# State space operators built in the first mixer's stage instead of the first, with norm sums and modulation steps in turn

## Chip, core and metric

The program runs on one NeuronCore of a Trainium2 chip. The time is the device time of one execution in microseconds (us), median over several. A profiled execution gives the trace; its engines are PE (TensorE matmul) and PEld (its weight loads), DVE (VectorE), ACT (ScalarE), POOL (GpSimd) and SP (SyncE, which here only issues DMAs; ACT and POOL issue some too).

## What is computed

Two networks run one after the other on 256 tokens of width 1024, all in float32. The first has two transformer blocks with adaptive modulation, the second an S5 state space block and an attention block. The parts that matter here are these:

```python
# first network, block i: modulation from the condition, for latent and context tokens
mod = silu(c) @ ada_w[i] + ada_b[i]            # 1024 x 6144; six vectors sh1 sc1 ga1 sh2 sc2 ga2
u   = rms_norm(h, g_mix[i]) * (1 + sc1) + sh1  # input of the mixer (block 0: neighborhood attention)
h   = h + ga1 * (mixer(u) @ wo)
h   = h + ga2 * squared_relu_mlp(rms_norm(h, g_mlp[i]) * (1 + sc2) + sh2)

# second network, S5 mixer: 64 groups of 16 channels, 64 complex states
a_bar = exp(lam * dt)                          # per group and state
b_bar = ((a_bar - 1) / lam)[..., None] * b_mat
s_t   = a_bar * s_{t-1} + b_bar u_t            # scan over the tokens
y_t   = real(c_mat s_t) + d_skip * u_t
```

The S5 scan is computed over chunks of eight tokens. For that the kernel builds operators from `lam`, `dt`, `b`, `c` and `d` alone, independent of the tokens: powers of `a_bar` times `b_bar` (`e`), their transposes (`et`), the short convolution kernel `c a^k b` with `d` on its diagonal (`k1`, `k2`), and some more.

## The kernel before, in words

Every product of the two networks is a float32 product split in two: a weight part of 128 x 1024 is loaded into `raw` (L266, L268), ACT rounds it to `whi` (L109), DVE subtracts to get `wlo` (L112), and PE runs three matmuls per pair of tiles (L294 to L296, or L302 to L304). `whi` and `wlo` have four buffers each, `raw` two.

Stages follow each other as blocks of `_build`, each with its own pools in SBUF and PSUM:
- The first stage (L936 to L1020) loads inputs and constants, sets up S5 (`S5.__init__` L599, `tables` L689, `c` L704), transposes x and ctx into `h` and `hc` (L983), runs 16 modulation steps (`ada`, `ada_steps` L345: load 128 x 1024 of `ada_w`, four matmuls L360 into one PSUM tile; at the eighth step of each vector a copy to `adacc`, two transposes and the bias), computes the norm's sums (`rstd` L442: eight squares, each summed by matmuls L428), and normalises (`normed` L466: per tile `t` on DVE, `xh` on ACT, `xl` on DVE). It also builds the operators for r = 0 to 3: `e(r)` is twelve DVE instructions, `operators(r)` is `k1`, `et` and `k2` on PE and ACT; `et` writes to DRAM (`edr`). At its end `zero` and `k_out` (16 DMAs of SP) write the convolution kernel to DRAM (`kdr`), and `save` some setup (`cdr`).
- From L975 to L1010 stands `tc.manual_schedule`: inside, every engine's instructions keep the order of the program. Outside, the framework orders them with its own planner, which may move an instruction of an engine past others; the eight `spread` DMAs (L794), written in the MLP's stage at L1259, are issued from 169.5 us on, in the attention's stage.
- The first mixer (L1028 to L1197) interleaves chains of scores and softmax with the products of the next head pair and with modulation steps; the bias tiles `bt` are loaded by SP from `rpad` (L1125).
- The next stage (L1240 to L1269) has the rest of the mixer's output product, the second norm of the block, the MLP on 512 tokens (32 weight tiles, after each of which two modulation steps run), and the S5 work that needs no tokens: `reload` of the setup from `cdr` on SP behind a small POOL instruction that waits for the last `h`, `phases` and sixteen `f` on POOL, and `spread`.
- The S5 layer itself (L1494 on) loads `edr`, `fdr`, `tdr` and `vdr`.

Of the kernel before, what the change touches and what calls it, by code (L numbers as in the profile page):

```python
# [17 lines left out]
KT = 8  # L18
# [64 lines left out]
def _build(ctx, tc, I, out, dbg):  # L83
# [337 lines left out]
    def rstd_rows(n, pooled=6, late=KT - 2):  # L421
# [20 lines left out]
    def rstd(n, pooled=6, late=KT - 2, tag="x"):  # L442

        return spread_cols(rstd_rows(n, pooled, late), n, tag)
# [123 lines left out]
    cdr = dram.tile([128, 1632], F32, name="cdr")  # L568
# [6 lines left out]
    def s5_load(pp):  # L575
        lt = spare(4, "lt")[0:32].rearrange("p (i n) -> p i n", i=4)
        ld = pp.tile([32, 2], F32, name="ld")
        dr = pp.tile([32, 32], F32, name="dr")
        bt = [[pp.tile([128, 1024], F32, tag=f"e{1 + r}{j}", name=f"bt{r}{j}")[0:32] for j in range(2)]
              for r in range(2)]  # L580
        ci = [pp.tile([128, 1024], F32, tag=f"e3{i}", name=f"ci{i}").rearrange("p (b d n) -> p b d n", b=8, d=2)
              for i in range(2)]
# [3 lines left out]
        for r, nm in ((0, "a_b_re_2"), (1, "a_b_im_2")):  # L586
            for j in range(2):
                todo.append((bt[r][j], I[nm][0].rearrange("(g j) p h -> g j (p h)", j=2)[:, j]))
# [3 lines left out]
        todo.append((dr, I["a_d_2"][0].rearrange("(a b) -> a b", b=32)))  # L592
        return (lt, ld, dr, bt, ci), [
            lambda o=o, i=i, n=n: (G.dma_start if 7 <= n < 11 else dma_a)(out=o, in_=i) for n, (o, i) in enumerate(todo)]

    class S5:


        def __init__(self, pp, loads):  # L599
            self.pp = pp  # L600
            lt, ld, dr, bt, ci = loads
# [11 lines left out]
            for r in range(2):  # L613
                for j in range(2):
# [15 lines left out]
            def sin_arg(t1, x, t0):  # L630
# [17 lines left out]
            cbs = spare(5, "cbk")  # L648
            G.memset(cbs, 0.0)
            self.cbk = [cbs[:, 256 * i:256 * i + 256].rearrange("p (q a b h) -> p q a b h", q=4, a=2, b=2)  # L650
                        for i in range(2)]
# [34 lines left out]
            self.ci, self.dr = ci, dr  # L686
            self.u, self.t_ = [(cs, sn), (s_[7], s_[8])], (t0, t1)

        def tables(self):  # L689
# [9 lines left out]
            self.em = [[pp.tile([128, 1024], F32, tag=f"e{r}{i}", name=f"e{r}{i}").rearrange(  # L699
                "p (q j t h) -> p q j t h", q=4, j=2, t=8) for i in range(2)] for r in range(3)]  # L700
            self.tm = [spare(2 + i, f"tm{i}").rearrange("p (n t h) -> p n t h", n=4, t=8) for i in range(2)]
            self.kt = [None] * 4

        def c(self):  # L704
            pp, ct, ci, dr = self.pp, self.ct, self.ci, self.dr
# [10 lines left out]
            for r in range(2):  # L716
                act(self.pf_[:, r], self.pw[r][:, 1:9, :], AF.Copy)
            self.dd = dd = pp.tile([32, 32, 32], F32, name="dd")
            pdk = bank("s")
            T.transpose(pdk[0:32, 0:32], dr, ident[0:32, 0:32])  # L720
            act(dr, pdk[0:32, 0:32], AF.Copy)
            tt(dd, dr.unsqueeze(2).to_broadcast([32, 32, 32]), ident[0:32, 0:32].unsqueeze(1).to_broadcast([32, 32, 32]),
               MUL)
            self.kst = [spare(10 + i, f"kst{i}").rearrange("p (r q j x) -> p r q j x", r=4, q=2, j=2) for i in range(2)]
            self.em.append([pp.tile([128, 1024], F32, tag=f"e3{i}", name=f"e3{i}").rearrange(
                "p (q j t h) -> p q j t h", q=4, j=2, t=8) for i in range(2)])

        def save(self):
# [12 lines left out]
        def k1(self, r):  # L741
# [6 lines left out]
            kp = bank("s")  # L748
# [9 lines left out]
            self.kt[r] = kt_ = self.pp.tile([128, 256], F32, tag="kt", name="kt", bufs=2)  # L758
# [13 lines left out]
        def k2(self, r):  # L772
            pk = bank("s")
# [24 lines left out]
        def reload(self, fp):  # L798
            c = fp.tile([128, 1632], F32, name="c")
            tt(c[:, 0:1], h[KT - 1][:, 0:1], hc[KT - 1][:, 0:1], ADD, G)  # L800
# [3 lines left out]
            self.ph = c[:, 1536:1632].rearrange("p (i g) -> p i g", i=3)  # L804

# [118 lines left out]
    with ExitStack() as sa:  # L924
# [11 lines left out]
        with ExitStack() as s0:  # L936
# [32 lines left out]
            def operators(r):  # L969
                s5.k1(r)  # L970
                s5.et(r)
                s5.k2(r)

# [928 lines left out]
```

## Time and profile before

| | us |
|---|---|
| median of three runs (1772.63 to 1781.13) | 1774.6 |
| the profiled execution | 1774.26 |
| its span, first to last instruction | 1772.5 |
| PE busy in the span | 1684.8 (95%) |
| DVE, ACT, POOL busy | 1177.6, 797.4, 445.7 |

A row of the timeline tells when an instruction (or a run of equal ones) started, how long it took, engine, source line, operation, output tile <- input tiles and shape; in brackets the idle time of the engine before it and what ended that. A row of the stretches tells the busy time of each engine in a window, the number of instructions, the granted clock of PE as a share of full, and the share of the 16 DMA engines. Matmuls are pipelined: their lengths overlap, so the distance of two starts tells what one of them costs.

### The profile page before, as it was taken

To read this page: it belongs to the slowest core of one execution; us is meant where nothing else is said; L and a number is where in the kernel's file an instruction comes from. 1 tells how busy PE (TensorE), PEld (TensorE's weight loads), DVE (VectorE), ACT (ScalarE), POOL (GpSimd) and SP (SyncE) were. 2 spreads that over 40 slices of the span, in tenths; PEclk is the share of its full clock that TensorE was granted. 3 is DMA by queue.
4 is the path that set the end of the run, shared out by engine and by line. 5 is a ranking of instruction groups with operands and counts; after the bars stand their busy time and mean duration, and the time that the engine had idled before them with its cause. 6 is when DMAs were issued, how large, how long until landed. Compare 5 with 4: busy or idle time off the path is not lost. (4 is left out here: it accounts for less than half of the span.)

```text
span 1772.5 us, 33896 instructions
## 1 busy us (share of the span) xinstructions
PE 1684.8 (95%) x13257; PEld 1485.2 (84%) x13257; DVE 1177.6 (66%) x2412; ACT 797.4 (45%) x1463; POOL 445.7 (25%) x619
## 2 busy tenths in 40 slices
PE   6899999999999999998998999989899999999999
PEld 5687888876677777888878999979899999789998
DVE  6877777855545333447985756768577788957674
ACT  5544444434323131324674635536444465544453
POOL 4022112146897000040002000221431322424130
PEclk9899999999999999999999999999999999999999
DMA  9566455333766555332206666698459574335952
GB/s 283 180 161 193 123 153 169 91 112 130 238 197 214 160 173 151 87 95 72 84 25 167 189 187 186 209 310 228 129 149 247 146 224 143 108 103 166 233 160 90
DMA packets 428288, 286.57 MB, mean 162 GB/s; under 512 B 37513, under 2 KB 405336, under 8 KB 428128
## 3 DMA queue, kind: packets, MB, share of 16 engines
q1 hardware_dynamic: 422064, 271.53, 52.8%
q0 software_dynamic: 2800, 7.29, 1.3%
q10 hardware_dynamic: 3264, 5.59, 0.9%
q8 instruction: 104, 1.70, 0.4%
q14 instruction: 56, 0.46, 0.1%
HBM read 271.41 MB, written 17.15 MB: 163 GB/s over the span
## 5 line engine op out<-in xcount | busy, mean ns | idle before, releaser
L109 ACT ACTIVATE whi<-raw 128x1024 fp32r<-128x1024 f32 (+2 forms) x388 | 390.1, 1013 | 470.4 <-PE g L295 361.5
L112 DVE TENSOR_TENSOR wlo<-raw,whi 128x1024 fp32r<-128x1024 f32 (+2 forms) x388 | 466.1, 1207 | 186.3 <-ACT whi L109 182.7
L296 PE MATMUL g<-xh,wlo 128*128 128x256 f32 (+1 forms) x1216 | 372.8, 307 | 8.0 <-DVE wlo L112 8.0
L294 PE MATMUL g<-xh,whi 128*128 128x256 f32 (+1 forms) x1216 | 371.9, 307 | 1.6 <-ACT xh L109 1.2
L295 PE MATMUL g<-xl,whi 128*128 128x256 f32 (+1 forms) x1216 | 371.5, 305 | 0.0
L294 PE MATMUL g<-oh,whi 128*128 128x256 f32 (+1 forms) x1056 | 333.2, 316 | 3.5 <-ACT oh L109 1.4
L296 PE MATMUL g<-oh,wlo 128*128 128x256 f32 (+1 forms) x1056 | 333.0, 315 | 0.0
L295 PE MATMUL g<-ol,whi 128*128 128x256 f32 (+1 forms) x1056 | 332.6, 315 | 0.4 <-DVE ol L112 0.4
L296 PEld LDWEIGHTS g<-xh,wlo 128*128 128x128 f32 x1216 | 232.2, 191 | 21.5 <-DVE wlo L112 10.2
L294 PEld LDWEIGHTS g<-xh,whi 128*128 128x128 f32 x1216 | 231.6, 191 | 17.6 <-ACT whi L109 3.9
L295 PEld LDWEIGHTS g<-xl,whi 128*128 128x128 f32 x1216 | 231.8, 191 | 10.9
L294 PEld LDWEIGHTS g<-oh,whi 128*128 128x128 f32 x1056 | 198.2, 188 | 24.2 <-issue 3.7
L295 PEld LDWEIGHTS g<-ol,whi 128*128 128x128 f32 x1056 | 198.3, 188 | 15.8 <-DVE ol L112 1.2
L296 PEld LDWEIGHTS g<-oh,wlo 128*128 128x128 f32 x1056 | 199.4, 189 | 14.3 <-issue 0.2
L302 PE MATMUL g<-whi,xh 128*128 128x256 f32 x560 | 163.1, 292 | 3.9 <-ACT whi L109 1.6
L303 PE MATMUL g<-wlo,xh 128*128 128x256 f32 x560 | 157.9, 282 | 0.1
L304 PE MATMUL g<-whi,xl 128*128 128x256 f32 x560 | 156.9, 283 | 0.2 <-DVE xl L115 0.2
L115 DVE SCALAR_TENSOR_TENSOR h<-g,mods,h 128x256 f32<-128x256 f32 x64 | 30.9, 483 | 142.2 <-PE g L296 142.2
L302 PEld LDWEIGHTS g<-whi,xh 128*128 128x128 f32 x560 | 105.9, 189 | 12.8 <-issue 8.7
L109 ACT ACTIVATE oh<-t 128x256 fp32r<-128x256 f32 (+1 forms) x108 | 51.3, 482 | 124.4 <-DVE t L112 124.4
L303 PEld LDWEIGHTS g<-wlo,xh 128*128 128x128 f32 x560 | 105.9, 189 | 0.8 <-issue 0.3
L304 PEld LDWEIGHTS g<-whi,xl 128*128 128x128 f32 x560 | 105.4, 189 | 1.3 <-issue 0.8
(329 smaller groups left out, 2823.4 us busy)
## 6 DMA issues: line engine op xcount, KB each, us to landing
raw<-mlp_w SPq DMA_DIRECT2D x128, 512.0 KB, 4.3
ada<-ada_w SPq DMA_DIRECT2D x88, 512.0 KB, 5.0
raw<-ffn_w_up SPq DMA_DIRECT2D x88, 512.0 KB, 5.2
raw<-ffn_w_down SPq DMA_DIRECT2D x32, 384.0 KB, 3.8
raw<-ffn_w_down SPq DMA_DIRECT2D x32, 320.0 KB, 3.4
raw<-na_wqkv SPq DMA_DIRECT2D x32, 256.0 KB, 5.0
raw<-a_w_glu SPq DMA_DIRECT2D x16, 512.0 KB, 7.2
raw<-w_kv SPq DMA_DIRECT2D x16, 512.0 KB, 3.7
```

What stands on the lines that cost most here:

```text
L109: last[0] = A.activation(out=o, in_=i, func=f, **kw)
L112: (e or V).tensor_tensor(out=o, in0=a, in1=b, op=op)
L115: V.scalar_tensor_tensor(out=o, in0=a, scalar=s, in1=b, op0=op0, op1=op1)
L294: T.matmul(ps, lhsT=a, rhs=xh[k][:, s0:s1], start=first, stop=False)
L295: T.matmul(ps, lhsT=a, rhs=xl[k][:, s0:s1], start=False, stop=False)
L296: T.matmul(ps, lhsT=b, rhs=xh[k][:, s0:s1], start=False, stop=last_)
L302: T.matmul(ps, lhsT=xh[k][:, t0:t0 + 128], rhs=a, start=first, stop=False)
L303: T.matmul(ps, lhsT=xh[k][:, t0:t0 + 128], rhs=b, start=False, stop=False)
L304: T.matmul(ps, lhsT=xl[k][:, t0:t0 + 128], rhs=a, start=False, stop=last_)
```

## The change

- In the first stage the operators are gone. It keeps the setup (`S5.__init__`, `tables`, `c`), and `save` now also writes `bb` and `pw2` to `cdr`, which grows from 1632 to 3168 columns. `b` is loaded with one DMA for each of its two parts (two before) and turned with 16 transposes each (16 transposes and 16 matmuls before). The loads of `c` and the small loads stand ahead of `tables`.
- `rstd` takes a function `between`, called after each of the eight sums: here it runs one modulation step each time, with `prep_vectors` at the fifth. Then `c`, four steps, the first weights, four steps. The second weights are loaded behind.
- `normed` of the first mixer now stands inside the hand-ordered section.
- `reload` stands at the head of the stage that holds the output product and the MLP. It loads the larger `cdr` without the POOL instruction that waited for `h`, loads `d` and builds `dd`, and allocates the operators' tiles: one `em` for all r, two `et` in turn (four before).
- `e(0)` follows `reload`; `k1`, `et` and `k2` of r = 0 stand behind the output product, ahead of the norm. Those of r = 1 to 3 hang on modulation steps of the MLP: `e` at steps 24, 32 and 40, the others four to six steps later, `k_out` at step 47; the eight `spread` follow behind all modulation steps.

```diff
@@ rstd_rows
+            if between:
+                between()
@@ S5.__init__
-                for j in range(2):
-                    b_ = bt[r][j].rearrange("g (p h) -> g h p", h=16)
-                    for h_ in range(16):
-                        o_ = pb[r][64 * j:64 * j + 64, 32 * h_:32 * h_ + 32]
-                        if j:
-                            T.matmul(o_, lhsT=b_[:, h_, :], rhs=ident[0:32, 0:32])
-                        else:
-                            T.transpose(o_, b_[:, h_, :], ident[0:32, 0:32])
+                b_ = bt[r].rearrange("g (n h) -> g h n", h=16)
+                for h_ in range(16):
+                    T.transpose(pb[r][:, 32 * h_:32 * h_ + 32], b_[:, h_, :], ident[0:32, 0:32])
@@ S5.save
+            for i in range(2):
+                dma_a(out=cdr[:, 1632 + 512 * i:2144 + 512 * i], in_=self.bb[i].rearrange("p g h -> p (g h)"))
+                dma_a(out=cdr[:, 2656 + 256 * i:2912 + 256 * i], in_=self.pw2[i].rearrange("p g t -> p (g t)"))
@@ S5.e
+            t = self.fp.tile([128, 2048], F32, tag="em", name="em").rearrange(
+                "p (i q j t h) -> p i q j t h", i=2, q=4, j=2, t=8)
+            self.em[r] = [t[:, i] for i in range(2)]
@@ S5.et
-                et = spare((0, 1, 4, 15)[q], "et").rearrange("p (j x) -> p j x", j=4)
-                pe = bank("s")
+                et = self.fp.tile([128, 512], F32, tag=f"et{q % 2}", name="et").rearrange("p (j x) -> p j x", j=4)
+                pe = bank("x")
@@ S5.reload
-            c = fp.tile([128, 1632], F32, name="c")
-            tt(c[:, 0:1], h[KT - 1][:, 0:1], hc[KT - 1][:, 0:1], ADD, G)
+            self.fp = fp
+            c = fp.tile([128, 3168], F32, name="c")
             dma(out=c, in_=cdr)
...
@@ first stage, inside manual_schedule
                 s5.tables()
-                for f in small_loads[15:-1]:
-                    f()
-                ada(4)
-                s5.c()
-                s5.e(0)
-                ada(2)
-                act(small, h[KT - 2][:, 0:1], AF.Sqrt, bias=eps, scale=0.0)
-                r_ = rstd(512, 0, None, "s")
-                prep_vectors(va)
-                ada(3)
-                s5.e(1)
-                operators(0)
-                ada(2)
-                w_first = [Weights(wpairs(w, D, 0), by_k=True)]
-                ada(2)
-                s5.e(2)
-                small_loads[-1]()
-                stt(gna, gna, 0.125, swg[:, 208:272], MUL, MUL)
-                ts(gsw[0], gsw[0], 0.125, MUL)
-                operators(1)
-                ada(3)
+                act(small, h[KT - 2][:, 0:1], AF.Sqrt, bias=eps, scale=0.0)
+                between = [lambda: ada(1)] * KT
+                between[4] = lambda: (prep_vectors(va), ada(1))
+                r_ = rstd(512, 0, None, "s", lambda: between.pop(0)())
+                s5.c()
+                ada(4)
+                w_first = [Weights(wpairs(w, D, 0), by_k=True)]
+                ada(4)
+                x = new_x(xa, "x", 512, 16, 16)
+                normed(x, r_, 512, lambda k, v: scg[0][:, 0, k, v:v + 1], lambda k, v: modcol(0, 0, k, v))
@@ first stage, behind it
+            small_loads[-1]()
+            stt(gna, gna, 0.125, swg[:, 208:272], MUL, MUL)
+            ts(gsw[0], gsw[0], 0.125, MUL)
             w_first.append(Weights(wcols(w, 2 * D, 256), by_k=True))
-            x = new_x(xa, "x", 512, 16, 16)
-            normed(x, r_, 512, lambda k, v: scg[0][:, 0, k, v:v + 1], lambda k, v: modcol(0, 0, k, v))
-            operators(2)
-            s5.e(3)
-            operators(3)
             s5.zero()
             s5.save()
-            s5.k_out()
@@ output product and MLP
+            s5.reload(fp)
+            s5.e(0)
             products(w_tiles(I["na_wo"][0], D, after=[ada_step])[2:], oT, KT, 512, ...
...
+            s5.k1(0)
+            s5.et(0)
+            s5.k2(0)
...
             mod_norm(x, 0, 3, 512)
-            s5.reload(fp)
...
-            ada_q[2::5] = [lambda f=f, s=s: (s5.spread(s), f()) for s, f in enumerate(ada_q[2:42:5])] + ada_q[42::5]
+            at_ = {24: lambda: s5.e(1), 32: lambda: s5.e(2), 40: lambda: s5.e(3), 47: s5.k_out}
+            for r in (1, 2, 3):
+                for i, f in enumerate((s5.k1, s5.et, s5.k2)):
+                    at_[20 + 8 * r + i] = lambda f=f, r=r: f(r)
+            for n, g_ in at_.items():
+                ada_q[n] = lambda f=ada_q[n], g_=g_: (f(), g_())
+            ada_q += [lambda s=s: s5.spread(s) for s in range(8)]
             mlp(0, 512, x, [ada_step, ada_step])
```

## Rows read from the trace of the kernel before

**Rows 1.** The page's first line.
```profile
span 1772.5 us, 33896 instructions
```
**Rows 2.** Timeline of PE, start: start, length, instruction, count.
```profile
66.57 0.61 PE L360 MATMUL x<-stl,sl 128*32 128x256 f32 x8
...
75.48 0.39 PE L302 MATMUL g<-whi,xh 128*128 128x256 f32 x1
```
**Rows 3.** Timeline of DVE, 70 to 127 us.
```profile
70.14 0.42 DVE L125 COPY adacc<-x 128x256 f32<-128x256 f32 x1
...
72.36 0.17 DVE L115 SCALAR_TENSOR_TENSOR scg<-mods,vt 128x16 f32<-128x16 f32 x1
...
73.08 0.47 DVE L115 SCALAR_TENSOR_TENSOR t<-h,scg,s 128x256 f32<-128x256 f32 x1
...
87.34 0.87 DVE L115 SCALAR_TENSOR_TENSOR xl<-t,mods,xh 128x256 fp32r<-128x256 f32 x2
...
98.20 1.07 DVE L513 TENSOR_REDUCE ss<-t 128x4 f32<-128x256 f32 x3 [2.52 <-ACT et L109]
...
126.47 0.42 DVE L112 TENSOR_TENSOR sc<-sc,bt 128x256 f32<-128x256 f32 x1
```
**Rows 4.** Timeline of SP's DMA issues, 49 to 112 us.
```profile
49.52 0.91 SPq L355 DMA_DIRECT2D stl<-ada_w  x2
...
99.38 12.09 SPq L790 DMA_DIRECT2D kdr<-kst  x16
```
**Rows 5.** Tile `stl` (modulation weights), 0 to 110 us: issue to landing.
```profile
DMA to landing us min/median/max: 4.1/5.4/12.0
```
**Rows 6.** Stretches: window, length, each engine's busy us (instructions), PE clock, DMA, GB/s.
```profile
40.00:44.00 4.00, 0.86 (x9) 0.84 (x8) 2.98 (x5) 1.99 (x7) 0.55 (x1) 0.90 1.14 346
...
52.00:56.00 4.00, 3.20 (x34) 1.98 (x37) 3.86 (x7) 2.39 (x5) 0.00 (x0) 1.00 0.91 345
```
**Rows 7.** Timeline of DVE and ACT, end of the second norm's `normed`.
```profile
424.30 0.47 DVE L115 SCALAR_TENSOR_TENSOR t<-hc,scg,x 128x256 f32<-128x256 f32 x1
...
424.81 0.51 ACT L109 ACTIVATE xh<-t,mods 128x256 fp32r<-128x256 f32 x1 [1.45 <-DVE t L115]
...
425.35 0.48 DVE L115 SCALAR_TENSOR_TENSOR xl<-t,mods,xh 128x256 fp32r<-128x256 f32 x1 [0.58 <-ACT xh L109]
```
**Rows 8.** Timeline of PE where it is dense, 90 to 98 us.
```profile
90.77 0.60 PE L767 MATMUL s<-cst,e 128*128 128x128 f32 x4
91.12 0.37 PE L304 MATMUL sc<-whi,xl 128*128 128x256 f32 x1
...
93.49 0.28 PE L303 MATMUL sc<-wlo,xh 128*128 128x256 f32 x1
...
96.34 0.65 PE L752 MATMUL s<-e,cbk 128*32 128x128 f32 x16
96.91 0.25 PE L756 MATMUL s<-cst,dd 32*32 32x16 f32 x8
97.09 0.66 PE L767 MATMUL s<-cst,e 128*128 128x128 f32 x4
```
**Rows 9.** Stretches: the second norm, the first MLP, the first mixer's early part.
```profile
405.00:425.00 20.00, 15.95 (x107) 11.07 (x106) 16.00 (x35) 8.77 (x20) 11.06 (x29) 0.91 0.59 198
480.00:500.00 20.00, 20.00 (x109) 14.87 (x108) 7.40 (x9) 3.38 (x4) 18.13 (x25) 1.00 0.74 237
125.00:150.00 25.00, 20.29 (x171) 13.79 (x169) 17.63 (x48) 12.41 (x32) 4.36 (x6) 0.93 0.62 192
```
**Rows 10.** Waits in 460 to 770 us: total us, times, longest.
```profile
ACT whi L109 <- PE g L295: 185.7, 51, 6.0
```
**Rows 11.** Line L770 (`et` to `edr`), 16 DMAs: issue to landing.
```profile
DMA to landing us min/median/max: 2.0/2.8/5.4
```
**Rows 12.** Groups by form, DVE, 33:97 and 460:560 us: busy us, mean ns.
```profile
L112 DVE TENSOR_TENSOR tm<-pz,bb 128x512 f32<-128x512 f32 x32 | 20.8, 685 | 0.3
...
L112 DVE TENSOR_TENSOR ol<-t,oh 128x512 fp32r<-128x512 f32 x8 | 9.9, 1244 | 5.3 <-ACT oh L109 5.3
```

More of the change, by code (lines that the diff above doesn't have):

```diff
@@ L419, in square_sum, with rstd_rows @@
                 yield acc
-    def rstd_rows(n, pooled=6, late=KT - 2):
+    def rstd_rows(n, pooled=6, late=KT - 2, between=None):
         w = n // 4
@@ L440, in spread_cols, with rstd @@
         return r
-    def rstd(n, pooled=6, late=KT - 2, tag="x"):
-        return spread_cols(rstd_rows(n, pooled, late), n, tag)
+    def rstd(n, pooled=6, late=KT - 2, tag="x", between=None):
+        return spread_cols(rstd_rows(n, pooled, late, between), n, tag)
     def rstd_cols(view=lambda v: v, pooled=6):
@@ L567, in _build @@
     vdr = dram.tile([3, 128, 1024], F32, name="vdr")
-    cdr = dram.tile([128, 1632], F32, name="cdr")
+    cdr = dram.tile([128, 3168], F32, name="cdr")
     rpad = dram.tile([240, 128], F32, name="rpad")
@@ L577, in s5_load @@
         ld = pp.tile([32, 2], F32, name="ld")
[L578 to L582, printed above, removed]
+        bt = [pp.tile([128, 2048], F32, tag=f"e{1 + r}", name=f"bt{r}")[0:32] for r in range(2)]
+        ci = pp.tile([128, 2048], F32, tag="e3", name="ci").rearrange("p (i b d n) -> p i b d n", i=2, b=8, d=2)
+        ci = [ci[:, i] for i in range(2)]
         todo = [(lt[:, 0, :], I["a_lam_re_2"][0].rearrange("(g j) p -> g (j p)", j=2)),
@@ L600, in __init__ @@
             self.pp = pp
-            lt, ld, dr, bt, ci = loads
+            lt, ld, bt, ci = loads
             self.ct = ct = [spare(12 + i, f"ct{i}").rearrange("p (g h) -> p g h", h=16) for i in range(2)]
@@ L697, in tables @@
                 cmul((ph[:, 0], ph[:, 1]) if i == 2 else u[(i + 1) % 2], u[i % 2], u[i % 2], self.t_)
[L699 to L702, printed above, removed]
         def c(self):
-            pp, ct, ci, dr = self.pp, self.ct, self.ci, self.dr
+            ct, ci = self.ct, self.ci
             for r in range(2):
@@ L717, in c @@
                 act(self.pf_[:, r], self.pw[r][:, 1:9, :], AF.Copy)
[L718 to L726, printed above, removed]
         def save(self):
@@ L747, in k1 @@
                     act(cbk[i][pj, :, :, j, :], cm, AF.Copy, scale=1.0 - 2.0 * i)
-            kp = bank("s")
+            kp = bank("x")
             for jp in range(2):
@@ L757, in k1 @@
                              rhs=C("dm")[0:32, :], start=False, stop=True)
-            self.kt[r] = kt_ = self.pp.tile([128, 256], F32, tag="kt", name="kt", bufs=2)
+            self.kt[r] = kt_ = self.fp.tile([128, 256], F32, tag="kt", name="kt")
             act(kt_, kp[:, 0:256], AF.Copy)
@@ L772, in k2 @@
         def k2(self, r):
-            pk = bank("s")
+            pk = bank("x")
             for jp in range(2):
@@ L804, in reload @@
             self.ph = c[:, 1536:1632].rearrange("p (i g) -> p i g", i=3)
+            self.bb = [c[:, 1632 + 512 * i:2144 + 512 * i].rearrange("p (g h) -> p g h", h=16) for i in range(2)]
+            self.pw2 = [c[:, 2656 + 256 * i:2912 + 256 * i].rearrange("p (g t) -> p g t", t=8) for i in range(2)]
+            self.em, self.kt = [None] * 4, [None] * 4
+            self.tm = [fp.tile([128, 512], F32, name=f"tm{i}").rearrange("p (n t h) -> p n t h", n=4, t=8)
+                       for i in range(2)]
+            cbs = fp.tile([128, 512], F32, name="cbk")
+            G.memset(cbs, 0.0)
+            self.cbk = [cbs[:, 256 * i:256 * i + 256].rearrange("p (q a b h) -> p q a b h", q=4, a=2, b=2)
+                        for i in range(2)]
+            self.kst = [fp.tile([128, 512], F32, name=f"kst{i}").rearrange("p (r q j x) -> p r q j x", r=4, q=2, j=2)
+                        for i in range(2)]
+            dr = fp.tile([32, 32], F32, name="dr")
+            dma(out=dr, in_=I["a_d_2"][0].rearrange("(a b) -> a b", b=32))
+            self.dd = dd = fp.tile([32, 32, 32], F32, name="dd")
+            pdk = bank("x")
+            T.transpose(pdk[0:32, 0:32], dr, ident[0:32, 0:32])
+            act(dr, pdk[0:32, 0:32], AF.Copy)
+            tt(dd, dr.unsqueeze(2).to_broadcast([32, 32, 32]), ident[0:32, 0:32].unsqueeze(1).to_broadcast([32, 32, 32]),
+               MUL)
         def phases(self, fp, hf):
@@ L967, in ada @@
                     ada_step()
[L969 to L972, printed above, removed]
             w = I["na_wqkv"][0]
             with tc.manual_schedule(engines={ENG.PE, ENG.DVE, ENG.Activation, ENG.SP, ENG.Pool}):
-                for f in vloads[0:2] + [lambda: dma(out=cst, in_=I["cst"])] + sloads[0:7] + xloads + small_loads[0:15]:
+                for f in vloads[0:2] + [lambda: dma(out=cst, in_=I["cst"])] + sloads[0:5] + xloads + small_loads[0:15]:
                     f()
```

18 lines of the change are left out of this document (7 added, 11 removed).

## The prediction

> **What bounds the kernel now.** I read four views in this order. The page's first lines give the span, 1772.5 us [rows 1]. The busy time by stretches says where PE is the limit: in 480 to 500 us, inside the first MLP, PE is busy 20.00 of 20 us, while DVE does 7.40 and ACT 3.38 [rows 9]. An instruction added to PE there lengthens the kernel by its own time. The start is the opposite. PE's timeline shows the first product of the first mixer only at 75.48 us [rows 2]; until then the kernel loads, builds modulation vectors (16 `ada` steps) and the state space operators. What releases that product? Its input `x` needs `scg`, ready at 72.36 + 0.17 = 72.53 us, which needs the copy `adacc` of the last modulation step at 70.14 us [rows 3]. The weights of that step were issued by SP until 49.52 + 0.91 = 50.43 us [rows 4], and loads of that tile take 4.1 to 5.4 us at the least and in the median [rows 5], so they were there at 54.5 to 55.8 us. The step's product ran at 66.57 us [rows 2]. So 11 to 12 us before it and 3 us behind it are not waiting for data: they are the hand-written order, in which `operators(0)`, `operators(1)`, `e(1)` and `e(2)` stand ahead of it on PE, ACT and DVE. A second queue follows: `x` is complete at 87.34 + 0.87 = 88.21 us, but the first `head_scale` reduction runs at 98.20 us [rows 3], with `e(3)` and `operators(3)` in between.
>
> **The part that gains: the start.** After the change no operator stands ahead of the modulation steps, so the last step is bound by its load. The transfers do not get much lighter: the DMA share is 1.14 in 40 to 44 us and 0.91 in 52 to 56 us [rows 6]; the same weights have to come. Three or four `edr` writes of 0.26 MB leave this stretch, and `save` adds 0.79 MB for `bb` and `pw2`. I therefore take the landing at 54 us, with 50 (at 345 GB/s [rows 6] the 1.3 MB that might be ahead or not are 4 us) to 58 us as ends, the upper one because each step now waits for a square and its sum on PE before its buffer is loaded again. Then 0.61 us of product [rows 2] and 72.53 - 70.14 = 2.39 us from the copy to `scg` [rows 3]: the first `t` of `normed` stands at 57.0 us instead of 73.08 us, a gain of 16.1 us.
>
> Part of it is given back. `normed` moves inside the hand-ordered section, so DVE has to keep program order: `t`, then `xl`, which waits for ACT's `xh`. One such triple that stood alone ran from 424.30 us over 424.81 us to 425.35 us, and its `xl` takes 0.48 us [rows 7]: 1.53 us for each of 16, 24.5 us in all. Before, the 32 DVE instructions ran interleaved in 88.21 - 73.08 = 15.1 us [rows 3]. PE's work on `x` meanwhile is 192 matmuls; twenty of them start between 91.12 and 93.49 us [rows 8], 0.118 us each, so 22.7 us: PE is fed, but does not finish early. Behind `x` there were 98.20 - 88.21 = 10.0 us to the reduction; now only the last products, one square and two `wlo` splits, which I take at 3.5 us. The reduction comes at 57.0 + 24.5 + 3.5 = 85.0 instead of 98.20 us: 13.2 us gained, with the landing's ends 9 to 17 us.
>
> The attention behind it gains a little more. `k_out` held SP for 12.09 us from 99.38 us [rows 4]; the bias loads stand behind it, and the first biased score is formed only at 126.47 us [rows 3], after which PE is busy 20.29 of 25 us in 125 to 150 us [rows 9]. With `k_out` gone the bias is early, chains and products can interleave, and of these 4.7 us, with a bit more from the low clock there (0.93 of full in the same row), 0 to 6 us come back; I take 3. Gain of the start: 16.2 us, ends 9 to 23. The shorter `b` transposes and the fewer `b` DMAs are worth nothing of their own: the loads end later than they do.
>
> **The part that costs: building the operators later.** Per `r` on PE, from the spacing of starts where PE is dense: four `et` transposes take 91.12 - 90.77 = 0.35 us, so sixteen 1.4; 16 of the 32 `k1` instructions take 96.91 - 96.34 = 0.57 us, so 1.14; eight small ones for `dd` take 97.09 - 96.91 = 0.18 us, so 0.36 [rows 8]; the two of `k2` some 0.2. Sum 3.1 us. Before, those of r = 2 and 3 also lay on a dense PE, which is already in the 98.20 us. Now r = 1, 2 and 3 lie inside the MLP, where nothing hides them: 9.3 us. The operators of r = 0 stand before `mod_norm`; PE is idle there for 20 - 15.95 = 4.05 us of 405 to 425 us [rows 9], so they cost 0 to 3.1 us; 1.5, since ACT must empty four banks for `et` in the midst of the norm's own chain.
>
> DVE: `e(r)` is twelve instructions of 0.685 us [rows 12], 8.2 us each, and `dd` once. Its cover is DVE's idle time, 12.6 of 20 us in the MLP [rows 9]. What could be late next is a weight split. But ACT waits 51 times, 185.7 us in all, for PE to give back a weight buffer [rows 10]: the splits run a buffer's use ahead of PE, so a delay of some us is absorbed. Nothing, then; without that cover 3 x 8.2 us.
>
> `et` now turns over two tiles instead of four. The copy into `et` for q = 2 must wait until the write of q = 0 has landed, 2.8 us in the median, 2.0 to 5.4 [rows 11]. That stops ACT, and PE only where its next instruction wants that bank: 0 to 2 us for each of three r; I take 1.5 in all.
>
> SP and DMA: `reload` brings 1.62 MB instead of 0.84 MB, 2.3 us more at 345 GB/s [rows 6], now ahead of the last `na_wo` loads instead of behind the norm; `k_out`'s 16 issues (12.09 us of SP [rows 4]) and the eight `spread` DMAs go into SP's order between MLP weights; 3.1 MB of `edr` writes share the queues. The same lead of the loads covers them [rows 10]: 0 to 4 us, taken at 1. The wait of `reload` for the last `h` and its POOL instruction go; POOL's `phases` may start earlier, and nobody waits for them until the state space layer.
>
> Cost: 9.3 + 1.5 + 1.5 + 1 = 13.3 us, ends 9 to 22.
>
> **Sum.** The profiled execution took 1774.3 us around its span of 1772.5 us, 0.3 us under the median of 1774.6 us. 1774.6 - 16.2 + 13.3 = 1771.7 us: a change within 0.5% (8.9 us, about what a measurement of this kernel can tell from no change).
>
> **The rivals.**
> - Clearly faster. The landing is at 50 us (4 us more), the bias brings 6 us (3 more), and r = 0, the `et` tiles and SP cost nothing (4 less): 1771.7 - 11 = 1760.7 us. For it: the start's queue is real and the costs besides PE's 9.3 us are all bounded by idle time. Against it: the full DMA engines. Chance 0.36.
> - The loads come late. A step's buffer is loaded again only after PE has used it, and in the new order PE reaches step k only after square k. If the last load lands at 62 us, the gain shrinks by 8: 1779.7 us. Chance 0.07.
> - Slower: PE stops for the two `et` tiles. If the transposes of one r stand back to back in PE's order, PE waits twice per r for a write (2.8 us [rows 11]) and four times for ACT's copy, at least the 0.51 us that ACT takes for half as many elements [rows 7]: 7.6 us for each of three r, 23 us instead of 1.5: 1793 us. It decides from the point where the products placed between two groups of transposes are shorter than the landing. For it: in the old start PE did wait for these copies; against it: PE has other products ready. Chance 0.11.
> - Slower: DVE beside POOL. POOL is busy 18.13 of 20 us in 480 to 500 us [rows 9], and a DVE instruction of `e`'s size with both inputs in SBUF takes 1.244 us there, against 0.685 us for `e` in the old start [rows 12], where POOL ran nothing (52 to 56 us [rows 6]). If `e(0)` and `e(1)` both fall beside POOL's work and PE waits for them, 2 x 12 x 0.56 = 13.4 us are added: 1785 us. Against it: nobody needs `e(r)` at once. Chance 0.06. The Trainium skill, SBUF — State Buffer, in its part on the engine side's shared port pair, states it as a rule: a VectorE instruction with two SBUF inputs and a GpSimd one that reads SBUF exclude each other for the whole instruction. The trace agrees in sign (0.685 against 1.244 us), not in a full exclusion for every instruction.
>
> **How the numbers follow.** My forecast, 1771.7 us, has 0.40 and its own range is 1765 to 1779 us. Faster than 0.5%: 0.36; within: 0.40 + 0.07 = 0.47; slower: 0.11 + 0.06 = 0.17. The range takes in the faster rival with 3 us below it, and the port rival above: 1757 to 1786 us; outside lie the `et` rival and the ends that add up.
>
> **What would show it.** Right: the last `adacc` copy of the start at 54 to 56 us, the first mixer product at 57 to 60 us with DVE alternating `t` and `xl`, the first `head_scale` reduction at 82 to 88 us, the attention stage ending some 16 us earlier, and the MLP some 10 to 12 us longer with PE still at its full 20 of 20. Wrong: a first product after 63 us (the loads bind), PE idle before `et` transposes in the MLP, or DVE instructions of 1.2 us with PE waiting for `wlo` or `em`.

## The result and the profile after

The changed kernel takes 1825.3 us in the median (1821.9 to 1829.0, four runs) against 1773.9 us for the kernel before (four runs, 1772.6 to 1781.1): ratio 1.028, 95% interval 1.025 to 1.032. The forecast was 1771.7 us, a change within 0.5%; the measured time is 54 us above it and outside its range of 1757 to 1786 us. The page's first line of the changed kernel answers [rows 1]:

```profile
span 1821.9 us, 33763 instructions
```

To see where the time went I cut both spans at four events that PE's timeline shows: the first product of the first mixer [rows 2], the end of the output product, the first MLP product, and the first sum of the next block's norm. These are the last three for the kernel before (start, length, instruction, count):

```profile
406.72 0.39 PE L296 MATMUL g<-oh,wlo 128*128 128x512 f32 x1
...
413.30 1.20 PE L294 MATMUL g<-xh,whi 128*128 128x512 f32 x4
...
805.78 0.43 PE L428 MATMUL x<-sq,cst 128*32 128x128 f32 x8
```

And all four after:

```profile
63.48 0.58 PE L302 MATMUL g<-whi,xh 128*128 128x256 f32 x1 [1.60 <-ACT xh L109]
...
389.56 0.39 PE L296 MATMUL g<-oh,wlo 128*128 128x512 f32 x1
...
427.37 1.26 PE L294 MATMUL g<-xh,whi 128*128 128x512 f32 x4
...
852.42 0.43 PE L428 MATMUL x<-sq,cst 128*32 128x128 f32 x8
```

Each stage is the difference of two of them (the output product ends 0.40 us behind its last start). The runs of the section below are cut in the same way. Each row of stages comes from one execution, and executions of one kernel lie some us apart (those of the kernel before from 1768 to 1779 us in the largest set of runs below), so a difference of 3 us in one stage is not much:

| us | start | attention and output product | norm | MLP | rest | span | median time |
|---|---|---|---|---|---|---|---|
| before | 75.5 | 331.6 | 6.2 | 392.5 | 966.7 | 1772.5 | 1773.9 |
| after | 63.5 | 326.5 | 37.4 | 425.1 | 969.5 | 1821.9 | 1825.3 |
| difference | -12.0 | -5.1 | +31.2 | +32.6 | +2.8 | +49.4 | +51.4 |

So the start gave what was forecast (12.0 + 5.1 = 17.1 us against 16.2), and the norm and the MLP grew by 64 us, where 13 had been reckoned.

**The start.** DVE's timeline of the changed kernel, answering [rows 3]:

```profile
27.02 0.20 DVE L120 TENSOR_SCALAR swg<-swg 128x64 f32<-128x64 f32 x1 [13.66 <-DMA swg<-swa_q_gain]
...
60.72 0.42 DVE L125 COPY adacc<-x 128x256 f32<-128x256 f32 x1 [6.03 <-PE x L360]
...
62.41 0.48 DVE L115 SCALAR_TENSOR_TENSOR t<-h,scg,s 128x256 f32<-128x256 f32 x1
...
87.05 0.48 DVE L115 SCALAR_TENSOR_TENSOR xl<-t,mods,xh 128x256 fp32r<-128x256 f32 x1 [0.58 <-ACT xh L109]
...
87.51 0.75 DVE L515 TENSOR_REDUCE ss<-t 128x4 f32<-128x256 f32 x2
...
104.35 0.43 DVE L112 TENSOR_TENSOR sc<-sc,bt 128x256 f32<-128x256 f32 x1 [0.84 <-PE sc L1126]
```

The first `t` comes at 62.41 instead of 73.08 us, the first reduction at 87.51 instead of 98.20, the first biased score at 104.35 instead of 126.47. The first row is new: the scaling of `gsw`, which stands behind the hand-ordered section in the text, was put ahead of DVE's S5 work by the planner, and DVE stood 13.66 us for a small load. ACT shows what followed:

```profile
22.34 0.29 ACT L109 ACTIVATE small<-h,cst 128x1 f32<-128x1 f32 x1
29.27 0.36 ACTq L709 DMA_DIRECT2D cdr<-bb  x1
31.34 0.42 ACT L109 ACTIVATE t<-h 128x256 f32<-128x256 f32 x1 [8.71 <-DVE bb L112]
```

A write of `save` had been put ahead of the norm's squares on ACT. It waits for `bb`, which DVE makes behind its own wait, so the first square came at 31.34 us, and with it the modulation steps that now follow each sum. The loads of later steps wait until earlier steps give back their buffers (SP stood 8.3 us for PE), so they were late too: the last one was issued at 52.31 us and landed at 59.56 us.

**The norm.** The norm sums the squares of eight tiles; six of them are made on POOL. In the kernel before, POOL's last squares came first and the instruction that waits for the last `h` behind them:

```profile
398.76 1.29 POOL L112 TENSOR_TENSOR sq<-sq,t 128x512 f32<-128x512 f32 x1
408.20 1.14 POOL L112 TENSOR_TENSOR c<-h,hc 128x1 f32<-128x1 f32 x1 [8.14 <-DVE hc L115]
```

PE's timeline and POOL's, changed kernel:

```profile
391.39 1.09 PE L748 MATMUL x<-cst,em 128*128 128x128 f32 x8
399.36 2.07 PE L748 MATMUL x<-cst,em 128*128 128x128 f32 x8 [6.88 <-ACT kt L109]
401.22 0.63 PE L756 MATMUL x<-cst,kt 128*128 128x128 f32 x2
419.66 0.65 PE L428 MATMUL x<-sq,cst 128*32 128x128 f32 x8 [17.81 <-POOL sq L112]
```
```profile
416.46 0.59 POOL L827 DMA_DIRECT2D vdr<-rt  x1 [0.36 <-POOL rt L826]
417.07 0.62 POOL L112 TENSOR_TENSOR t<-h 128x256 f32<-128x256 f32 x1
417.64 0.62 POOL L112 TENSOR_TENSOR t<-hc 128x256 f32<-128x256 f32 x1
418.34 1.26 POOL L112 TENSOR_TENSOR sq<-sq,t 128x512 f32<-128x512 f32 x1
```

PE waits 17.81 us for the sum of squares on POOL. POOL's last squares stand behind the writes of `vdr`: `phases` ran between the squares, from 360.17 us on. The 6.88 us before it have the same source: PE waited for `kt`, which stood on ACT behind a square that waited 5.62 us for a buffer of POOL's `sq`.

**The MLP's end.** Stretches of the changed kernel (columns as in [rows 9]), then SP's issues and ACT's work there:

```profile
740.00:820.00 80.00, 66.14 (x253) 50.75 (x252) 25.51 (x32) 20.16 (x27) 1.56 (x3) 0.91 0.44 125
```
```profile
738.21 1.25 SPq L775 DMA_DIRECT2D tdr<-kdr  x2
739.55 1.05 SPq L268 DMA_DIRECT2D raw<-mlp_w  x1
740.64 4.56 SPq L775 DMA_DIRECT2D tdr<-kdr  x2
745.30 17.52 SPq L268 DMA_DIRECT2D raw<-mlp_w  x2
```
```profile
747.17 0.60 ACT L109 ACTIVATE t<-g 128x512 f32<-128x512 f32 x1 [10.33 <-PE g L296]
...
752.70 0.60 ACT L109 ACTIVATE t<-g 128x512 f32<-128x512 f32 x1 [3.55 <-PE g L296]
...
758.24 0.60 ACT L109 ACTIVATE t<-g 128x512 f32<-128x512 f32 x1 [3.55 <-PE g L296]
...
760.13 1.04 ACT L109 ACTIVATE whi<-raw 128x1024 fp32r<-128x1024 f32 x1
```
```profile
761.22 0.51 PE L294 MATMUL g<-xh,whi 128*128 128x512 f32 x1 [3.02 <-ACT whi L109]
```

PE is busy 66 of 80 us. SP's last loads of weights are mixed with `spread` (L775). The load issued at 739.55 us landed at 746.66 us (3.8 to 7.1 us for `raw` here), but its split `whi` ran only at 760.13 us, 13.5 us later, and PE waited for it. The split itself waited for nothing: ACT had three copies `t` ahead of it, each of which waits for PE.

### The profile page after: what moved, and what is told of

Same layout as the page of the kernel before. It is cut to its first block, busy times and chain, and to the rows that moved or that the text cites. A ratio compares the mean times of both kernels' runs of the same rounds, so it can differ in the third digit from the quotient of the medians.

```text
span 1821.9 us, 33763 instructions
## 1 busy us (share of the span) xinstructions
PE 1690.0 (93%) x13193; PEld 1484.2 (81%) x13193; DVE 1178.9 (65%) x2412; ACT 799.2 (44%) x1463; POOL 446.8 (25%) x618
## 5 line engine op out<-in xcount | busy, mean ns | idle before, releaser
L112 POOL TENSOR_TENSOR sq<-h 128x256 f32<-128x256 f32 x7 | 5.4, 775 | 411.5 <-DVE h L115 384.9
```

The lines of the kernel that those rows point to most:

```text
L112: (e or V).tensor_tensor(out=o, in0=a, in1=b, op=op)
```

## The experiments

**1. Is the norm late for POOL?** One POOL instruction is added to the changed kernel, so that `phases` waits for the last `h`, as `reload` did before.

```diff
             tb = fp.tile([128, 2, 16, 16], F32, tag="ft", name="tb")
+            if hf == 0:
+                tt(vt_[0][:, 0, 0:1], h[KT - 1][:, 0:1], hc[KT - 1][:, 0:1], ADD, G)
```

> The changed kernel with one small POOL instruction more: ahead of `phases` a POOL addition reads the last `h` and `hc`, so that `phases` and `f` can only start when the output product is done, as in the kernel before. Theory A (POOL): in the changed kernel the planner put `phases` ahead of the norm's squares on POOL, and the norm's sum waits 17.8 us for it; ACT's last squares wait behind the same buffers (9.6 us). Then the first MLP product comes 18 to 28 us earlier than 427.4 us and the time falls from 1825 to 1797 to 1807 us. Theory B (operators of r = 0): the norm is late because k1, et and k2 of r = 0 stand ahead of it on PE and ACT. Then the first MLP product stays after 420 us and the time stays at 1817 us or above.

Measured: 1804.7 us, ratio to before 1.0175 (1.0159 to 1.0191); the norm took 13.9 us instead of 37.4, the first MLP product came at 402.23 us. Theory A holds: 23.5 us of the norm are POOL's order. (The time fell by 20.6 us; MLP and rest were 2.3 and 3.7 us longer in this execution.) Theory B, the operators of r = 0, is left with the other 7.7 us (13.9 against 6.2), to which 5 and 8 come back.

**2. The same line alone, in the kernel before.**

```diff
             c = fp.tile([128, 1632], F32, name="c")
-            tt(c[:, 0:1], h[KT - 1][:, 0:1], hc[KT - 1][:, 0:1], ADD, G)
```

> The kernel before with one line less: the POOL addition in `reload` that waits for the last `h`. Everything else is as before. Theory A (POOL): `phases` then stands ahead of the norm's squares 4 and 5 on POOL; the norm's gap of 6.2 us on PE grows by 10 to 25 us and the time rises from 1774 to 1784 to 1799 us. Theory B (operators of r = 0 cause the late norm): no change within 5 us of 1774 us.

Measured: 1782.3 us, ratio 1.0054 (1.0034 to 1.0073), 9.5 us more than the 1772.8 us of the kernel before, measured beside it. That is just under theory A's range of 1784 to 1799 us, and outside theory B's 5 us; the norm took 15.0 us instead of 6.2. Without anything else of the change, PE waits for the same thing:

```profile
415.24 0.65 PE L428 MATMUL x<-sq,cst 128*32 128x128 f32 x8 [7.30 <-POOL sq L112]
```

**3. `k_out` and `spread` off SP.** In the changed kernel both are issued by POOL.

```diff
-                    dma(out=kdr[:, 32 * qh:32 * qh + 32, 7 + s, :],
+                    G.dma_start(out=kdr[:, 32 * qh:32 * qh + 32, 7 + s, :],
...
-            dma(out=tdr[16 * s:16 * s + 16],
+            G.dma_start(out=tdr[16 * s:16 * s + 16],
```

> The changed kernel with the 16 DMAs of `k_out` and the eight of `spread` issued by POOL instead of SP. Theory C (SP's order): the MLP took 425.1 us instead of 392.5, of which 9.3 are the operators on PE; the other 23 us are weight loads that stand on SP behind `k_out` and behind `spread`, which waits for `k_out` to land. Then 14 to 23 us come back: 1802 to 1811 us, with PE at 20 of 20 between 740 and 820 us. Theory D (the DMA engines or ACT's copies hold the MLP's end, whoever issues): no change, 1820 us or above, with PE at 15 to 18 of 20 there.

Measured: 1801.6 us, ratio 1.0161 (1.0143 to 1.0180), a hair below theory C's range; the MLP took 403.7 us instead of 425.1, and in the same stretch PE was full:

```profile
740.00:820.00 80.00, 80.00 (x347) 64.63 (x346) 35.55 (x45) 23.90 (x31) 21.47 (x22) 1.00 0.49 146
```

Theory C's sum holds, and theory D falls. Of the 21.4 us, 80 - 66.14 = 13.9 us were idle time of PE. Much of the rest goes with the granted clock, which was 0.91 in that stretch behind PE's waits and is 1.00 here: by estimate 0.09 x 66.1 = 6 us. Whether SP's time is the cause is tested in 7.

**4. The small items of the start.** `small_loads[-1]`, the two scalings, `zero` and `save` go inside the hand-ordered section, behind `normed`.

```diff
                 normed(x, r_, 512, lambda k, v: scg[0][:, 0, k, v:v + 1], lambda k, v: modcol(0, 0, k, v))
-            small_loads[-1]()
-            stt(gna, gna, 0.125, swg[:, 208:272], MUL, MUL)
-            ts(gsw[0], gsw[0], 0.125, MUL)
+                small_loads[-1]()
+                stt(gna, gna, 0.125, swg[:, 208:272], MUL, MUL)
+                ts(gsw[0], gsw[0], 0.125, MUL)
+                s5.zero()
+                s5.save()
             w_first.append(Weights(wcols(w, 2 * D, 256), by_k=True))
-            s5.zero()
-            s5.save()
```

> The changed kernel with `small_loads[-1]`, the two scalings of `gna` and `gsw`, `zero` and `save` inside the hand-ordered section, behind `normed`. Theory E: outside it the planner put the scaling (a 13.66 us wait of DVE for a small load) and the writes of `bb` (on ACT's queue, ahead of the norm's squares) early, so the squares came at 31.3 us and with them the modulation steps that follow each sum. Then the last `adacc` copy comes at 50 to 57 us instead of 60.72 us, and the time falls by 3 to 10 us, to 1815 to 1822 us. Theory F (the loads of `ada` bind the start whatever the order): the copy stays at 59 us or later and the time within 3 us of 1825 us.

Measured: 1825.2 us, ratio 1.0292 (1.0275 to 1.0309): no gain, although the last `adacc` copy came at 48.06 us instead of 60.72 and the first product at 50.57 us instead of 63.48. So the loads bound the start only through the order ahead of them (F falls), and theory E is right in the place and wrong in the time. The writes of `save` now stood on ACT ahead of the mixer's copies, and DVE's first reduction waited for them:

```profile
77.15 1.42 ACTq L710 DMA_DIRECT2D cdr<-pz  x1
78.67 1.21 ACT L109 ACTIVATE t<-g 128x256 f32<-128x256 f32 x4 [4.56 <-DMA cdr<-pz]
```
```profile
81.31 1.07 DVE L515 TENSOR_REDUCE ss<-t 128x4 f32<-128x256 f32 x3 [6.44 <-DMA cdr<-pz]
```

The output product ended at 386.8 instead of 390.0 us, and the MLP, which the edit doesn't touch, was 3.8 us longer (428.9 us) in this execution; why is open.

**5. Together, and r = 0.** The edits of 1 and 3 in one kernel; then k1, et and k2 of r = 0 moved into the MLP.

```diff
-            s5.k1(0)
-            s5.et(0)
-            s5.k2(0)
...
-            for r in (1, 2, 3):
+            for r in (0, 1, 2, 3):
                 for i, f in enumerate((s5.k1, s5.et, s5.k2)):
```

> The changed kernel with both edits that each gave 21 to 24 us: the POOL addition ahead of `phases`, and `k_out` and `spread` issued by POOL. Theory (A and C are two independent losses, one in the norm, one at the MLP's end): they add up; from the stages of the two runs, 62.1 + 326.2 + 13.9 + 403.7 + 968.6 = 1774.5 us of span, so a time of 1776 to 1783 us. Rival (the second hides part of the first, as weight loads that came early behind a late norm): 1785 to 1800 us.

> As the run with both edits, and k1, et and k2 of r = 0 moved from ahead of the norm to the modulation steps 20 to 22 of the MLP. Theory G (r = 0 lengthens the norm's gap): with the POOL addition alone the gap of PE was 13.9 us instead of 6.2; ACT held the norm's square root behind an `et` copy that waited for a DMA. The gap returns to 6 to 7 us, the MLP takes 3 us more: 3 to 6 us less than the run with both edits. Rival (the gap is longer for another reason): the gap stays above 11 us and the time does not fall.

Measured: 1777.9 us for both edits, ratio 1.0030 (1.0018 to 1.0041): the losses are independent and add up. With r = 0 in the MLP 1781.2 us, ratio 1.0047 (1.0028 to 1.0066): the norm is back at 6.2 us, as theory G said, but the time did not fall: the MLP grew from 403.6 to 411.9 us, not by 3. By the distances of their starts k1, et and k2 of r = 0 took 3.6 us of PE there; PE's waits in 500 to 600 us (total, times, longest) name 4.6 more of these 8.3 us:

```profile
PE x L367 <- DVE adacc L125: 4.6, 1, 4.6
```

Ahead of that copy `adacc` DVE ran `e(1)`, beside a POOL that was busy 20.34 of 24 us (524 to 548 us). Pairs of `tm` took 1.91 to 2.08 us there.

And why were 13.9 us of norm left after experiment 1? There ACT had `sd`, the norm's square root, behind an `et` copy that waited 2.46 us for a DMA. Four `et` tiles remove that wait:

```diff
-                et = self.fp.tile([128, 512], F32, tag=f"et{q % 2}", name="et").rearrange("p (j x) -> p j x", j=4)
+                et = self.fp.tile([128, 512], F32, tag=f"et{q}", name="et").rearrange("p (j x) -> p j x", j=4)
```

> The run with both edits (1777.9 us), and four `et` tiles instead of two. Theory J: two tiles make ACT wait for a DMA ahead of the norm's square root (2.46 us there) and 17.1 us in three waits in the MLP, where the lead of the weight splits hides them; with four the norm's gap falls from 14.0 to 10 to 12 us and the time by 1 to 4 us, to 1774 to 1777 us. Rival (the two tiles cost PE their waits in the MLP too): the MLP falls from 403.6 to below 397 us and the time by more than 8 us. Second rival: no change at all, within 1 us.

Measured: 1778.1 us, ratio 1.0028 (1.0015 to 1.0041), against 1777.9 with two tiles, and the norm still 14.0 us. Theory J falls and the second rival, no change, is right: with ACT's wait gone, DVE was next, with `e(1)` ahead of the norm's reciprocal, and PE waited 4.08 us for that:

```profile
393.45 0.37 ACT L109 ACTIVATE sd<-x,cst 128x128 f32<-128x128 f32 x1
```
```profile
395.55 0.69 DVE L112 TENSOR_TENSOR em<-tm,tm 128x512 f32<-128x512 f32 x1
396.15 0.95 DVE L434 RECIPROCAL sd<-sd 128x128 f32<-128x128 f32 x1
```
```profile
397.16 2.07 PE L441 MATMUL x<-sd,cst 128*128 128x128 f32 x8 [4.08 <-DVE sd L434]
```

The other 4 us are PE's own: from the first `k1` at 387.57 to the end of `k2` at 391.13 + 0.44 us.

**6. The start, freed.** On top of r = 0 in the MLP: the small items inside the section, with `save` on POOL's queue. Other than in 4, `small_loads[-1]`, `zero` and `save` stand ahead of `normed` here, and only the two scalings behind it. Then the same with `normed` outside the section.

```diff
@@ save, its eight writes
-                dma_a(out=cdr[:, 512 * i:512 * i + 512], in_=self.ct[i].rearrange("p g h -> p (g h)"))
+                G.dma_start(out=cdr[:, 512 * i:512 * i + 512], in_=self.ct[i].rearrange("p g h -> p (g h)"))
...
@@ first stage, the second of the two kernels
-                normed(x, r_, 512, lambda k, v: scg[0][:, 0, k, v:v + 1], lambda k, v: modcol(0, 0, k, v))
+            normed(x, r_, 512, lambda k, v: scg[0][:, 0, k, v:v + 1], lambda k, v: modcol(0, 0, k, v))
```

> As the run before it, and in the first stage `small_loads[-1]`, `zero`, `save` and the scaling of `gna` and `gsw` inside the hand-ordered section, with the eight writes of `save` on POOL's queue instead of ACT's. Theory H: with them inside but on ACT's queue the first product came 8.6 us earlier (54.85 us), and the first reduction only 6.2 us, because it waited 6.44 us for the writes of `pw2`; on POOL's queue that wait goes and the first reduction comes at 75 to 79 us instead of 87.5; the time falls by 4 to 12 us against the run before it. Rival (behind the first product the attention stage is bound by PE or by its loads): the output product ends as early as before within 3 us, and the time stays.

> As the run before it, with `normed` of the first mixer outside the hand-ordered section. Theory I: inside, DVE alternates `t` and `xl` in 16 serial triples of 1.53 us (24.6 us measured); free, they take some 15 us; PE needs 22.7 us for its products of x, so the first reduction comes 2 to 9 us earlier and the time falls by 0 to 6 us. Rival (the planner's order moves other work ahead of `x`, as it did with the scaling): the first product or the reduction comes later, and the time rises.

Measured: 1776.9 us, ratio 1.0025 (1.0011 to 1.0039), then 1765.9 us, ratio 0.9956 (0.9941 to 0.9970). Of theory H 4.3 us came, the low end of its range; the first reduction came at 80.58 us, later than expected, and the output product ended 3.5 us earlier, just past the rival's 3. The first product came at 55.32 us, against 50.57 us in experiment 4 (the 54.85 us of the expectation are a later row of that run). The eight writes now ran from 40.0 to 45.5 us, beside the last weight loads: one issued at 41.41 us landed 8.2 us later, where one issued at 41.74 us in experiment 4 took 4.9 us. That the writes slowed it is likely, not shown. Of theory I 11.0 us came, more than expected. DVE with `normed` inside the section, then outside:

```profile
54.24 0.48 DVE L115 SCALAR_TENSOR_TENSOR t<-h,scg,s 128x256 f32<-128x256 f32 x1
55.30 0.49 DVE L115 SCALAR_TENSOR_TENSOR xl<-t,mods,xh 128x256 fp32r<-128x256 f32 x1 [0.58 <-ACT xh L109]
...
80.58 0.74 DVE L515 TENSOR_REDUCE ss<-t 128x4 f32<-128x256 f32 x2
```
```profile
53.43 0.47 DVE L115 SCALAR_TENSOR_TENSOR t<-h,scg,s 128x256 f32<-128x256 f32 x1
53.82 0.47 DVE L115 SCALAR_TENSOR_TENSOR t<-hc,scg,s 128x256 f32<-128x256 f32 x1
54.21 0.47 DVE L115 SCALAR_TENSOR_TENSOR t<-h,scg,s 128x256 f32<-128x256 f32 x1
54.61 1.27 DVE L115 SCALAR_TENSOR_TENSOR xl<-t,mods,xh 128x256 fp32r<-128x256 f32 x3
...
69.54 1.06 DVE L515 TENSOR_REDUCE ss<-t 128x4 f32<-128x256 f32 x3
```

Inside, nearly every `xl` stands right behind its `t` and waits 0.58 us for ACT; the 32 instructions take 26 us. Outside, several `t` run ahead, and the 32 take 14 us. The attention and output product end 12.2 us earlier (373.1 against 385.3 us).

**7. SP's time or ACT's order?** The changed kernel with only `spread` on POOL, and with only `k_out` on POOL: one half each of the diff of 3.

```diff
-            dma(out=tdr[16 * s:16 * s + 16],
+            G.dma_start(out=tdr[16 * s:16 * s + 16],
```
```diff
-                    dma(out=kdr[:, 32 * qh:32 * qh + 32, 7 + s, :],
+                    G.dma_start(out=kdr[:, 32 * qh:32 * qh + 32, 7 + s, :],
```

> The changed kernel with only the eight DMAs of `spread` on POOL; the 16 of `k_out` stay on SP. Theory L (ACT's order): the loads stood on SP behind `spread`, so the planner reckoned them late and put ACT's weight splits `whi` behind the copies `t` and `oh`; ACT then waited for PE (10.33 us at 747 us) with landed weights behind it. Without `spread` on SP the splits stand ahead again: the MLP falls from 425.1 us to 402 to 408 us, 17 to 23 us in all, though `k_out` still holds SP for 8.4 us. Rival M (SP's own time): the gain is in proportion to the issue time taken off, 8 to 12 us: an MLP of 413 to 417 us.

> The changed kernel with only the 16 DMAs of `k_out` on POOL; the eight of `spread` stay on SP. Theory L (ACT's order): `spread` still stands ahead of weight loads, ACT's splits stay behind the copies for the most part: 0 to 8 us less than 1825 us, an MLP of 417 to 425 us. Rival M (SP's own time): 8 to 12 us less, an MLP of 413 to 417 us.

Measured: `spread` moved 1807.7 us, ratio 1.0197 (1.0175 to 1.0218), MLP 408.3 us; `k_out` moved 1816.8 us, ratio 1.0253 (1.0231 to 1.0275), MLP 415.1 us. The first agrees with theory L (its MLP a hair above the range) and is out of the rival's; the second is out of theory L's MLP range and lies in the rival's. The shares, 16.8 and 10.0 us, are together more than the 21.4 us of both edits, so neither proportion explains them. The rows favour ACT's order. With `k_out` still holding SP for 8.57 us from 727.75 us, only 2.15 us of PE were lost in 740 to 760 us. With `spread` on SP, PE lost 3.6 us each in 760 to 780 and in 780 to 800 us. SP had issued two loads of weights by 756.2 us, and ACT had four copies `t` ahead of their two splits, of which this is the last:

```profile
752.73 3.46 SPq L268 DMA_DIRECT2D raw<-mlp_w  x2
```
```profile
774.70 0.60 ACT L109 ACTIVATE t<-g 128x512 f32<-128x512 f32 x1 [3.55 <-PE g L296]
776.05 0.63 ACT L109 ACTIVATE oh<-t 128x512 fp32r<-128x512 f32 x1 [0.76 <-DVE t L112]
776.59 1.99 ACT L109 ACTIVATE whi<-raw 128x1024 fp32r<-128x1024 f32 x2
```

The two loads landed at 760.24 and 761.76 us, some 15 us ahead of their splits, so in this stretch PE did not wait for SP's time but for ACT's order. What made that order is open: an order of ACT changed by hand, with SP's left as it is, was not tried. That the planner put the splits back because it reckoned the loads late is the reading that fits, not shown.

**8. The parts that helped, together.** The edits of 1 and 3, the start of 6 with `normed` outside, four `et` tiles, r = 0 ahead of the norm; then r = 0 one weight tile earlier, inside the output product:

```diff
+            def wo_step():
+                ada_step()
+                n_[0] += 1
+                if n_[0] == 3:
+                    s5.k1(0)
+                    s5.et(0)
+                    s5.k2(0)
...
-            s5.k1(0)
-            s5.et(0)
-            s5.k2(0)
```

> All edits that helped: POOL addition ahead of `phases`; `k_out`, `spread` and `save` on POOL's queue; the small items of the first stage inside the hand-ordered section, `normed` outside; four `et` tiles; r = 0 ahead of the norm, as in the changed kernel (not in the MLP, where it took 8 us instead of 3). From the stages: 54.5 + 318.6 + 11 + 403 + 969 = 1756 us of span, so 1755 to 1763 us; rival (r = 0 costs the same at either place): 1764 to 1768 us.

> As the run before it, with k1, et and k2 of r = 0 one weight tile earlier, between the last products of the output product, where PE is dense and POOL does only the norm's squares. Theory G: there they cost PE's own 3.1 us and no wait: the norm's gap returns to 6 to 7 us, the output product takes 3 to 4 us more, 1 to 3 us less in all than the run before it. Rival: ACT's copies delay the weight splits or the squares and the time is the same or up to 3 us longer.

Measured: 1766.8 us, ratio 0.9960 (0.9945 to 0.9975), in the range of the rival. By stages r = 0 is still cheaper ahead of the norm (norm and MLP 14.2 + 402.8 = 417.0 us) than in the MLP (6.2 + 413.6 = 419.8), by less than the stages of single executions can settle; what is missing lies in the norm, 14.2 us instead of 11, and in the rest, 975.7 us instead of 969. Then 1762.0 us, ratio 0.9936 (0.9919 to 0.9952), faster than the kernel before by 11.7 us. Its stages are 55.5, 323.1, 6.2, 402.0 and 973.3 us: r = 0 costs 5.5 us in the output product and gives back 8.0 us in the norm. The gap of the norm is what theory G said; the time fell by 4.8 us, more than its 1 to 3 us, and 3.2 us of that lie in the MLP and the rest, which the edit does not touch.

## Why the prediction was wrong, step by step

- **The start's gain: right in size by luck, as errors cancelled.** Forecast 16.2 us, measured 17.1. The first `t` came at 62.41 us, 5.4 us later than the 57.0 taken, since the wait for `swg` and the `bb` write held the squares; experiment 4, where they don't, has the copy at 48.06 us, earlier than the landing's lower end. Given back was the tail behind `xl`, taken at 3.5 us: the reduction followed 0.46 us behind the start of the last `xl`. Behind the reduction the attention was to gain 3 us, 6 at most; it gained 17.1 - 10.7 = 6.4 us. The sign of being wrong, a first product after 63 us, did come (63.48 us), but the loads that it names were late only for the order ahead of them.
- **`normed` in hand order: right.** 24.5 us forecast, 62.41 to 87.53 us measured, 25.1. The forecast had it on the path, against 15.1 us in the kernel before; experiment 6 bears out those 9.4 us and a little more: with `normed` free the reduction came 11.0 us earlier and the time fell by 11.0 us. There this part of the change was a loss.
- **Operators of r = 1 to 3: right.** With POOL and SP out of the way (experiment 5) the MLP takes 403.6 us, 11.1 more than before, where 10 to 12 us were forecast. By the distances of starts one r took PE 3.6 us there (1.48 for k1, 1.75 for et, 0.37 for k2) instead of the 3.1 summed up, so 10.8 us for three.
- **The failed step: "The wait of `reload` for the last `h` and its POOL instruction go; POOL's `phases` may start earlier, and nobody waits for them until the state space layer."** Nobody waits for `phases`, but the norm waits for the six squares on POOL, the later of which now stood among and behind them. 23.5 us (experiment 1), costed at nothing. The step looked only for who needs the moved work, not for what is queued behind it on its engine.
- **The second failed step: "The same lead of the loads covers them", 0 to 4 us, taken at 1, for `k_out` and `spread`.** 21.4 us (experiment 3). The lead of the splits that [rows 10] show belonged to one order of ACT. With DMAs among the loads ACT's order was another: landed weights lay 13.5 us unsplit while ACT waited for PE. That the planner made it for that reason is not shown (experiment 7).
- **r = 0 in the norm's gap:** 1.5 us forecast with 3.1 as the upper end, 7.8 measured (14.0 - 6.2 in experiment 5): 4 us of PE (3.1 forecast), which the gap did not hide because the norm's sum stands behind them, and about 4 us of waits on ACT and DVE.
- **The rivals.** The loads that come late were met in mechanism: the last one landed at 59.56 us, against 54 forecast and 62 in that rival, and the first `t` was 5.4 us late; its time, 1779.7 us, was not. PE did not stop for the two `et` tiles: in experiment 5 ACT waited 15.8 us in three waits for them in the MLP (the expectation of four tiles says 17.1), PE 0.5 us; with four tiles the MLP took 1.4 us less. DVE beside POOL may have a part in the 4.6 us of one arrangement (experiment 5): a pair of `tm` took 1.91 to 2.08 us there, 1.34 us in the norm of the run with four `et` tiles, beside less work of POOL. The Trainium skill's rule (SBUF — State Buffer, SBUF: two separate sides), by which a VectorE instruction with two SBUF inputs and a GpSimd one that reads SBUF exclude each other, agrees with the sign of that. In those 24 us DVE was busy 19.93 and POOL 20.34, together more than the stretch; but no row tells whether a recorded length holds a wait for the port, so the runs, and the 0.685 against 1.244 us of the prediction, neither confirm a full exclusion nor speak against it. The slower side, which had 0.17, came true by neither of its two mechanisms.
- **Sum.** From the stages before, after and in experiment 5: -17.1 + 11.1 + 21.5 (SP) + 23.4 (POOL) + 7.8 (r = 0) + 2.8 (rest) = 49.5 us, the 49.4 of the spans.

What stays open: the rest of the kernel, in which nothing was changed, took 1.3 to 9.0 us longer than the 966.7 us before in every run (968.0 to 975.7 us). With the same 8105 matmuls PE was busy 927.2 us in the longest and 921.4 before, at a granted clock of 0.97 and 0.98; what moves it is not known.

## What to carry to other kernels

When an instruction that makes others wait is taken away, list what then gets ahead on the same engine, and who waits for the work that it passes; that the moved work itself is not urgent says nothing. An order that a planner makes is not a fixed background: DMAs put among weight loads, or a small instruction that falls out of a hand-ordered part, can turn the order of other engines, so a lead read from one trace is no cover for a change of the queues. And a step that is already serial in a trace (`t`, `xh`, `xl`) is worth freeing where it feeds the limit.

## What was not expected of the hardware

Issuing from POOL cost the kernel nothing here, although it is no free work: in experiment 3 the 16 `k_out` DMAs took 9.98 us of POOL (8.42 us of SP in the changed kernel) and the eight `spread` 6.02 us (11.1 us of SP, between the loads). POOL was held from 728.0 to 745.0 us, its next work came at 790.1 us, and PE was busy 80 of 80 us. A write can hold engines that never read what it writes: `save`, whose data is first read by `reload` behind the mixer, held ACT's first copies for 4.56 us and DVE's first reduction for 6.44 us in experiment 4. The trace names the landing of `cdr<-pz` as the end of both waits. Whether the landing or ACT's queue held them is not separated: experiment 6, where the wait is gone, changed both the queue and the place of the writes.
